# Retention outputs turned by VectorE, stored by ScalarE and gated in the last stage; a chunk's states first

## The chip, the cores and the metric

The kernel runs on one core of one Trainium2 chip. The metric is device time in microseconds, lower is better. A core has engines that run their own instruction queues in order and wait for each other through semaphores: TensorE (PE; its weight loads are listed as PEld), VectorE (DVE), ScalarE (ACT), GpSimd (POOL) and SyncE (SP), which here issues most DMA transfers.

## The reference

One layer of a hybrid decoder for a prompt of 1024 tokens and 32 sampled tokens (8 sequences of 4), all float32. The part that matters here is the retention branch, 4 heads with keys of 256 and values of 512, over the prompt in chunks of 128 tokens:

```python
def retention_chunk(q, k, v, s_prev, log_g):
    ...
    scores = jnp.einsum('bihd,bjhd->bhij', q, k) * dmask[None]
    intra = jnp.einsum('bhij,bjhe->bihe', scores, v)
    ...
    cross = jnp.einsum('bihd,bhde->bihe', q, s_prev) * q_decay[None, :, :, None]
    ...
    s_new = (jnp.exp(c * log_g)[None, :, None, None] * s_prev
             + jnp.einsum('bjhd,bjhe->bhde', k * k_decay[None, :, :, None], v))
    return intra + cross, s_new

def retention_out(o, rg, gn_w):
    ...
    on = ((o - mu) * lax.rsqrt(var + EPS)).reshape(b, s, RET_VW).astype(rg.dtype)
    return on * gn_w * jax.nn.silu(rg)
```

The gated outputs go through a projection (`w_down_ret`) and are merged with the attention branch by sigmoid gates; an output projection, a residual and a second gated embedding follow.

## The kernel before

Each float32 product is computed as three matmuls of rounded halves (`mac`, L265 to L269): high by high, high by low, low by high. Every operand is therefore split, usually by a copy on ScalarE or GpSimd (`hi_pool`, L197) for the high half and a subtraction on VectorE (`lo_of`, L200) for the low half. TensorE is kept busy by weaving streams of matmuls: a generator yields the cost of what it has just emitted, and `woven` takes turns by those costs. The final order of the instructions on each engine is set by a scheduler from dependences and priorities.

The stages by time: projections and gates (0 to about 370 us; the retention gate, after its SiLU, goes to DRAM as `gtD`), the paged attention of the sampled tokens (to 745), retention (745 to 1320), the prompt's attention (to 1620), and the last stage, which projects both branches, merges them and ends the layer.

In retention, a head's `prompt_chunks` (L926 to L1023) goes over eight chunks. `values_of` (L877) makes a chunk's values: 24 matmuls of 128x512 into the buffer `mm` (two PSUM buffers), then `vnh` on ScalarE (L884) and `vnl` on VectorE (L200). `front` (L935) makes the scores (L939), masks them (`smr`, L942), splits them (`smh`, `sml`) and loads and splits the decayed keys (`knh`, `knl`). `back` (L957) makes the output `po` of the chunk: three inner-chunk matmuls (values by scores), six on the old state (`Sth`, `Stl` by the split queries `qch`, `qcl`), then two sets of three for the new state, whose result is added to `S` (L981) and split into `Sth` (GpSimd) and `Stl` (VectorE) for the next chunk. `group_norm` (L887 to L903) normalises `po`: `bn` and its aggregate, `gv`, then `gr` on GpSimd, `gs`, `gb`, and `on` on ScalarE (L902).

`gate_out` (L910) turns the 128x512 `on` on TensorE, by four transposes of 128x128 into PSUM (L915), or for the sampled tokens by a matmul with a selecting matrix (L917), multiplies by the weight and the gate, which SyncE loaded (`gate_in`, L905), in four VectorE operations (L919), and stores the result with SyncE to `goD` (L921). In a head's loop, the values of chunk c+1 are woven with what is left of chunk c−1 (the `due` generator) and the first part of chunk c, with budgets 5.5 and 3.9.

`sample_state` (L1037) does the same for the sampled tokens with 16 states; its `gate_out` is done at the start of the next head (`late`). While one head's chunks end, the next head's `head_qk` (L816) projects queries and keys and copies them out on ScalarE.

In the last stage, `gated` (L1476) loads 128 rows of `goD` over all 1056 tokens, and `split_gated` splits them into `gh` (ScalarE) and `gl` (VectorE, three pieces of 352). `w4` is a pool of three buffers of 128x1056, used for the sigmoid gates (L1493) and later for other things. The products of this stage are evacuated by VectorE, one 128x352 piece each 24 matmuls (L1510, L1515, and L1532 on).

Of the kernel before, what the change touches and what calls it, by code (L numbers as in the profile page):

```python
# [162 lines left out]
def decode_step(ctx: ExitStack, tc: tile.TileContext, A: dict, O: dict):  # L163
# [17 lines left out]
    def tr():  # L181
        return banks["pool"].tile([P, 512], F32, tag="tr", name="tr", bufs=3)
# [13 lines left out]
    def hi_pool(out, src):  # L196
        pool.tensor_scalar(out, src, 1.0, 1.0, op0=ALU.mult, op1=ALU.mult)  # L197
# [22 lines left out]
    gtD, goD = ([dram.tile([P, 4, NT], F32, tag=f"{n}{h}", name=f"{n}{h}") for h in range(HR)] for n in ("gt", "go"))  # L220
# [684 lines left out]
    def gate_in(h, n, cols):  # L905
        g = p4.tile([P, 4, P], F32, tag="g", name="g", bufs=3)[:, :, :n]
        sp.dma_start(g, gtD[h][:, :, cols])
        return g

    def gate_out(h, on, n, cols, g):  # L910
        pt = tr()
        for f in range(4):
            o = pt[:, f * P:f * P + n]
            if n == P:
                pe.transpose(o, on[:, f * P:(f + 1) * P], ident)  # L915
            else:
                pe.matmul(o, on[:, f * P:(f + 1) * P], C("sel"), start=True, stop=True)  # L917
        for f in range(4):
            dve.scalar_tensor_tensor(out=g[:, f, :], in0=pt[:, f * P:f * P + n], scalar=gnw[:, 4 * h + f:4 * h + f + 1],  # L919
                                     in1=g[:, f, :], op0=ALU.mult, op1=ALU.mult)  # L920
        sp.dma_start(goD[h][:, :, cols], g)  # L921
# [4 lines left out]
    def prompt_chunks(h, X):  # L926
# [30 lines left out]
        def back(c, parts):  # L957
            sl = slice(c * P, (c + 1) * P)
            smh, sml, kh, kl = parts
            vh, vl = V.pop(c)  # L960
            if c:
                qh, ql = pair("qc", DK, 1)
                for m in range(2):
                    ms = slice(m * P, (m + 1) * P)
                    hi_pool(qh[:, ms], q[m][:, sl])
                    lo_of(ql[:, ms], q[m][:, sl], qh[:, ms])
            g = gate_in(h, P, sl)
            po = ac()
            mac(po, (smh, sml), (vh, vl), True, c == 0)
            yield 0.65  # L970
            for m in range(2 if c else 0):
                Sh, Sl = T["S"]
                ms, vs = slice(m * P, (m + 1) * P), slice(m * DV, (m + 1) * DV)
                mac(po, (qh[:, ms], ql[:, ms]), (Sh[:, vs], Sl[:, vs]), False, m == 1)
                yield 0.65
            for m in range(2):
                ms, vs = slice(m * P, (m + 1) * P), slice(m * DV, (m + 1) * DV)
                pS = ac()
                mac(pS, (kh[:, ms], kl[:, ms]), (vh, vl), True, True)
                if c:  # L980
                    dve.scalar_tensor_tensor(out=S[:, vs], in0=S[:, vs], scalar=gC, in1=pS, op0=ALU.mult, op1=ALU.add)  # L981
                else:
                    act.copy(S[:, vs], pS)
                yield 0.65
            if c < 7:
                Sh, Sl = T["S"] = tuple(p4.tile([P, 2 * DV], F32R, tag="st", name=f"St{n}", bufs=4) for n in "hl")
                for m in range(2):
                    vs = slice(m * DV, (m + 1) * DV)
                    hi_pool(Sh[:, vs], S[:, vs])
                    lo_of(Sl[:, vs], S[:, vs], Sh[:, vs])  # L990
            on = group_norm(po, P, C("qd", h, 1), C("qd2", h, 1))
            yield None
            gate_out(h, on, P, sl, g)
            yield 0.43

# [10 lines left out]
        while late:  # L1006
            gate_out(*late.pop())
        due = iter(())
# [28 lines left out]
    def sample_state(h, X):  # L1037
# [3 lines left out]
        sl = slice(SEQ, NT)  # L1041
# [30 lines left out]
        yield 2.5  # L1072
# [28 lines left out]
        g = gate_in(h, NR, sl)  # L1101
# [24 lines left out]
        if h + 1 < HR:  # L1126
            late.append((h, on, NR, sl, g))
        else:
            gate_out(h, on, NR, sl, g)
            yield 0.5  # L1130
# [350 lines left out]
    def split_gated(hi, lo):  # L1481

        for j in range(3):
            sl = slice(j * TH, (j + 1) * TH)
            split(b32(lo)[:, sl], hi[:, sl], lo[:, sl])
        return hi, lo

    def load_gated(f, pl):
        lo = gated(f, pl)
        return split_gated(pl("gh"), lo)  # L1490
# [30 lines left out]
    gx[7] = split_gated(xr_("gh"), gx[7])  # L1521
# [298 lines left out]
```

## Time and profile before

| | |
|---|---|
| time, median of 3 runs | 2126.42 us (2119.92 to 2126.49) |
| the profiled execution: time, span | 2122.66 us, 2120.9 us |
| granted TensorE clock | 0.997 of full speed |
| TensorE busy in 745 to 780, 855 to 905 and 905 to 980 us | 35.00 of 35, 50.00 of 50, 75.00 of 75 |
| turning transposes (L915) | 128 instructions, 19.3 us busy |
| selecting matmuls (L917) | 32 records of 269 ns (two for each instruction) |
| gating operations of 128x128 (L919) | 128 instructions, 341 ns each |
| `on` (L902), `vnl` (L200) | 36 of 778 ns, 32 of 686 ns |
| load of the gate, store of the result, to landing | 3.2 us and 2.6 us for 256 KB |
| TensorE's listed waits in all | 18 causes, the longest 4.9 us, at the start |

A row of the timeline gives the start, the duration, the engine, the source line, the operation, output and inputs by the program's names, and in brackets how long the engine was idle before it and what ended that. Matmuls are pipelined: durations overlap, and it is the distance between starts that adds up. [...] A row of the groups ends with busy time, mean nanoseconds of one, and the idle time before such instructions with its releasers. A row of the windows gives the stretch, its length, the busy time and count of PE, PEld, DVE, ACT and POOL, the granted clock, the DMA share and GB/s.

### The profile page before, as it was taken

To read this page: it belongs to the slowest core of one execution; us is meant where nothing else is said; L and a number is where in the kernel's file an instruction comes from. 1 tells how busy PE (TensorE), PEld (TensorE's weight loads), DVE (VectorE), ACT (ScalarE), POOL (GpSimd) and SP (SyncE) were. 2 spreads that over 40 slices of the span, in tenths; PEclk is the share of its full clock that TensorE was granted. 3 is DMA by queue.
4 is the path that set the end of the run, shared out by engine and by line. 5 is a ranking of instruction groups with operands and counts; after the bars stand their busy time and mean duration, and the time that the engine had idled before them with its cause. 6 is when DMAs were issued, how large, how long until landed. Compare 5 with 4: busy or idle time off the path is not lost. (4 is left out here: it accounts for less than half of the span.)

```text
span 2120.9 us, 38551 instructions
## 1 busy us (share of the span) xinstructions
PE 2085.8 (98%) x15282; PEld 1806.3 (85%) x15282; DVE 1239.0 (58%) x2791; ACT 699.6 (33%) x1455; POOL 306.0 (14%) x517
## 2 busy tenths in 40 slices
PE   8999999999999999999999999999999999999998
PEld 7988777777777898888888887888888999999976
DVE  6524555565655457677676774877777353454443
ACT  6312232333433232222222222454566341232221
POOL 2210111111100022222222220122211000000000
PEclk9999999999999999999999999999999999999999
DMA  7576656566565332654635647210112453336642
GB/s 206 135 242 212 238 193 233 208 246 227 193 240 182 113 87 71 206 163 140 208 87 163 195 147 251 56 48 19 39 52 81 152 181 94 95 117 133 175 151 91
DMA packets 346870, 321.91 MB, mean 152 GB/s; under 512 B 126945, under 2 KB 294049, under 8 KB 342593
## 3 DMA queue, kind: packets, MB, share of 16 engines
q1 hardware_dynamic: 320192, 213.92, 34.5%
q0 software_dynamic: 9216, 83.89, 10.6%
q10 hardware_dynamic: 17280, 21.63, 2.8%
q8 instruction: 120, 1.97, 0.4%
q14 instruction: 62, 0.50, 0.1%
HBM read 246.69 MB, written 72.69 MB: 151 GB/s over the span
## 5 line engine op out<-in xcount | busy, mean ns | idle before, releaser
L267 PE MATMUL mm<-xh,wh 128*128 128x352 f32 x1344 | 456.7, 340 | 3.9 <-ACT gev L440 2.3
L269 PE MATMUL mm<-xh,wl 128*128 128x352 f32 x1344 | 436.5, 325 | 2.1 <-DVE wl L200 2.1
L268 PE MATMUL mm<-xl,wh 128*128 128x352 f32 x1344 | 436.6, 325 | 0.0
L267 PEld LDWEIGHTS mm<-xh,wh 128*128 128x128 f32 x1344 | 253.2, 188 | 87.4 <-issue 77.2
L269 PEld LDWEIGHTS mm<-xh,wl 128*128 128x128 f32 x1344 | 254.2, 189 | 3.9 <-DVE wl L200 2.4
L268 PEld LDWEIGHTS mm<-xl,wh 128*128 128x128 f32 x1344 | 254.3, 189 | 3.4 <-issue 2.1
L688 DVE STREAM_TRANSPOSE kt<-craw 128x512 f32<-128x512 f32 x256 | 161.3, 681 | 85.9 <-PE sc L692 81.1
L200 DVE TENSOR_TENSOR wl<-wr,wh 128x512 fp32r<-128x512 f32 (+2 forms) x203 | 139.3, 699 | 98.1 <-ACT wh L248 67.1
L248 ACT CAST wh<-wr 128x512 fp32r<-128x512 f32 x150 | 90.0, 618 | 240.5 <-PE mm L268 184.6
L440 ACT ACTIVATE gev<-mm 128x352 f32<-128x352 f32 x120 | 55.5, 463 | 238.8 <-PE mm L269 218.4
L267 PE MATMUL mm<-mh,wh 128*128 128x352 f32 x384 | 124.5, 324 | 1.4 <-ACT mh L1197 0.8
L268 PE MATMUL mm<-ml,wh 128*128 128x352 f32 x384 | 124.8, 325 | 0.8 <-DVE ml L200 0.6
L269 PE MATMUL mm<-mh,wl 128*128 128x352 f32 x384 | 124.3, 324 | 0.0
L269 PE MATMUL mm<-gh,wl 128*128 128x352 f32 x384 | 124.3, 324 | 0.0
L267 PE MATMUL mm<-gh,wh 128*128 128x352 f32 x384 | 124.3, 324 | 0.0
L268 PE MATMUL mm<-gl,wh 128*128 128x352 f32 x384 | 124.2, 323 | 0.0
L267 PE MATMUL mm<-wv,xh 128*128 128x512 f32 x256 | 103.5, 404 | 0.0
L268 PE MATMUL mm<-wv,xh 128*128 128x512 f32 x256 | 100.9, 394 | 0.0
L269 PE MATMUL mm<-wv,xl 128*128 128x512 f32 x256 | 100.8, 394 | 0.0
L692 PE MATMUL sc<-kt,q 32*32 32x512 f32 x2560 | 91.2, 600 | 0.0
L902 ACT ACTIVATE on<-ac,gb,gs 128x512 f32<-128x512 f32 x36 | 28.0, 778 | 153.1 <-DVE gb L900 147.9
L267 PEld LDWEIGHTS mm<-mh,wh 128*128 128x128 f32 x384 | 72.4, 188 | 1.9 <-ACT mh L1197 1.0
(419 smaller groups left out, 4365.6 us busy)
## 6 DMA issues: line engine op xcount, KB each, us to landing
wr<-in_w_in_dram SPq DMA_DIRECT2D x144, 256.0 KB, 3.7
st<-in_state_ret_dram SPq DMA_DIRECT2D x32, 512.0 KB, 5.1
out_ret_sample_dram<-st SPq DMA_DIRECT2D x32, 512.0 KB, 3.5
gt<-gev ACTq DMA_DIRECT2D x48, 176.0 KB, 3.1
gl<-go SPq DMA_DIRECT2D x16, 528.0 KB, 5.4
gate<-ga SPq DMA_DIRECT2D x16, 528.0 KB, 3.6
g<-gt SPq DMA_DIRECT2D x32, 256.0 KB, 3.2
go<-g SPq DMA_DIRECT2D x32, 256.0 KB, 2.6
```

What stands on the lines that cost most here:

```text
L200: dve.tensor_tensor(out=out, in0=src, in1=b32(hi), op=ALU.subtract)
L248: hi_by[0](hi, raw)
L267: pe.matmul(out, wh, xh, start=first, stop=False)
L268: pe.matmul(out, wh, xl, start=False, stop=False)
L269: pe.matmul(out, wl, xh, start=False, stop=last)
L440: act.activation(t, ps, func)
L688: dve.transpose(kt[:, 2 * i + s].rearrange("p (n r) -> p n r", r=32), src)
L692: pe.matmul(sc[32 * v:32 * v + 32, q, :], Q["q4"][qs_, j + v // 2, 2 * (g % 2) + v % 2, :], kt[qs_, v, :], start=n == 0, stop=n == NJ // 2 ...
L902: act.activation(on[:n], po, AF.Identity, bias=nb[:n], scale=s[:n])
```

## The change

1. `gate_in` and `gate_out` go. `turn_out` lets VectorE transpose `on` in blocks of 32x32 (one stream transpose of 128x512 from SBUF to SBUF), and `store_out` lets ScalarE store it in four transfers, one for each 32 tokens, in pieces of 128 bytes. `goD` has a layout that fits these blocks. TensorE, the PSUM buffer `tr` and SyncE take no part any more.
2. The store of a chunk is emitted one chunk later: `store_out` stands ahead of `turn_out`.
3. The gate is applied in the last stage: `gated` loads the rows of `goD` and the gate `rg` (a buffer of `w4`), and VectorE multiplies them with the weight over 128x1056 ahead of the split. 16 such loads and 16 such operations are new.
4. In `back` the matmuls for the new state come first, then the inner-chunk and the old-state matmuls for the output. The old state's halves are kept in `old`.
5. `front(1)`, the scores and keys of the second chunk, is emitted inside the woven loop of the first chunk, once its costs have passed 3.5. The budget of the chunk's remainder goes from 3.9 to 3.5, and a yield in `sample_state` from 2.5 to 3.5.

```diff
-    gtD, goD = ([dram.tile([P, 4, NT], F32, tag=f"{n}{h}", name=f"{n}{h}") for h in range(HR)] for n in ("gt", "go"))
+    gtD = [dram.tile([P, 4, NT], F32, tag=f"gt{h}", name=f"gt{h}") for h in range(HR)]
+    goD = [dram.tile([DV // 32, 32, NT], F32, tag=f"go{h}", name=f"go{h}") for h in range(HR)]
...
-    def gate_in(h, n, cols):
...
-    def gate_out(h, on, n, cols, g):
...
+    def turn_out(h, on, n, t0):
+        st = p4.tile([P, DV], F32, tag="g", name="g", bufs=3).rearrange("p (b r) -> p b r", r=32)
+        dve.transpose(st, on.rearrange("p (b r) -> p b r", r=32))
+        turned_out.append((h, st, n, t0))
+
+    def store_out():
+        while turned_out:
+            h, st, n, t0 = turned_out.pop(0)
+            for a in range(4):
+                act.dma_start(goD[h][:, :, t0 + a * n:t0 + a * n + n].rearrange("b i t -> i b t"), st[32 * a:32 * a + 32, :, :n])
...
-            g = gate_in(h, P, sl)
-            po = ac()
-            mac(po, (smh, sml), (vh, vl), True, c == 0)
-            yield 0.65
-            for m in range(2 if c else 0):
-                Sh, Sl = T["S"]
...
+            old = T.get("S")
             for m in range(2):
                 pS = ac()
...
+            po = ac()
+            mac(po, (smh, sml), (vh, vl), True, c == 0)
+            yield 0.65
+            for m in range(2 if c else 0):
+                Sh, Sl = old
...
             on = group_norm(po, P, C("qd", h, 1), C("qd2", h, 1))
             yield None
-            gate_out(h, on, P, sl, g)
-            yield 0.43
+            store_out()
+            turn_out(h, on, 32, c * P)
...
-                parts = front(c + 1)
-                yield 1.0
-                yield from woven((chain(due, ahead(u)), 3.9), (values_of(c + 1, X, V), 5.5))
+                if c:
+                    parts = front(c + 1)
+                    yield 1.0
+                both = woven((chain(due, ahead(u)), 3.5), (values_of(c + 1, X, V), 5.5))
+                for cost in both:
+                    yield cost
+                    if c == 0:
+                        done += cost
+                        if done > 3.5:
+                            parts, done = front(1), -99.0
+                            yield 1.0
...
-        yield 2.5
+        yield 3.5
...
         lo = pl("gl")
-        sp.dma_start(b32(lo), goD[f // 4][:, f % 4, :])
-        return lo
+        sp.dma_start(b32(lo), goD[f // 4][4 * (f % 4):4 * (f % 4) + 4].rearrange("b i t -> (b i) t"))
+        g = w4("rg", dt=F32)
+        sp.dma_start(g, gtD[f // 4][:, f % 4, :])
+        dve.scalar_tensor_tensor(out=g, in0=b32(lo), scalar=gnw[:, f:f + 1], in1=g, op0=ALU.mult, op1=ALU.mult)
+        return lo, g
```

TensorE's order in the middle of a head, from a chunk's scores on (`ac<-q,k`). Before, the transposes stand behind the scores, then the inner-chunk matmuls between values (`mm`) of the next chunk:

```order
3680 L939 MATMUL ac<-q_7994,k_8230 128x128
3681 L939 MATMUL ac<-q_7995,k_8231 128x128
3682 L915 MATMUL tr<-cst,on 128x128 x4
3683 L267 MATMUL mm<-wv,xh_113 128x512
3684 L268 MATMUL mm<-wv,xh_113 128x512
3685 L269 MATMUL mm<-wv,xl_114 128x512
3686 L267 MATMUL ac<-vnh,smh 128x512
3687 L268 MATMUL ac<-vnl,smh 128x512
3688 L269 MATMUL ac<-vnh,sml 128x512
```

Now, in the same place (`mac` stands one line lower, and the middle matmul of a product need not follow the first directly):

```order
3637 L935 MATMUL ac<-q_7994,k_8230 128x128
3638 L935 MATMUL ac<-q_7995,k_8231 128x128
3639 L268 MATMUL mm<-wv,xh_113 128x512
3640 L269 MATMUL mm<-wv,xh_113 128x512
3641 L268 MATMUL ac<-vnh,knh 128x512
3642 L270 MATMUL mm<-wv,xl_114 128x512
3643 L268 MATMUL mm<-wv,xh_115 128x512
3644 L269 MATMUL ac<-vnl,knh 128x512
3645 L270 MATMUL ac<-vnh,knl 128x512
```

The transposes are gone, and the state matmuls (`knh`) are the first to use `vnh` and `vnl`; the inner-chunk matmuls (`smh`) follow later. Of a product's three matmuls the one with `vnl` is put a few places back.

VectorE's order around the end of a chunk's output, in the middle of a head. Before, from the group norm's first operation on:

```order
593 L890 BN_STATS st_8890<-ac 128x6
594 L200 TENSOR_TENSOR qcl<-q_7994,qch 128x128
595 L892 BN_AGGR mv<-st_8890 128x2
596 L200 TENSOR_TENSOR qcl<-q_7995,qch 128x128
597 L894 TENSOR_SCALAR gv<-mv,cst 128x1
598 L981 SCALAR_TENSOR_TENSOR S<-S,ac 128x512
599 L898 TENSOR_TENSOR gs<-gr,cst 128x1
600 L900 SCALAR_TENSOR_TENSOR gb<-mv,gs 128x1
601 L200 TENSOR_TENSOR Stl<-S,Sth 128x512
602 L981 SCALAR_TENSOR_TENSOR S<-S,ac 128x512
603 L942 TENSOR_TENSOR smr<-ac,cst 128x128
604 L200 TENSOR_TENSOR vnl<-mm,vnh 128x512
```

Now:

```order
577 L891 BN_STATS st_8771<-ac 128x6
578 L200 TENSOR_TENSOR qcl<-q_7994,qch 128x128
579 L893 BN_AGGR mv<-st_8771 128x2
580 L200 TENSOR_TENSOR qcl<-q_7995,qch 128x128
581 L895 TENSOR_SCALAR gv<-mv,cst 128x1
582 L899 TENSOR_TENSOR gs<-gr,cst 128x1
583 L901 SCALAR_TENSOR_TENSOR gb<-mv,gs 128x1
584 L938 TENSOR_TENSOR smr<-ac,cst 128x128
585 L200 TENSOR_TENSOR vnl<-mm,vnh 128x512
586 L910 STREAM_TRANSPOSE g<-on 128x512
587 L200 TENSOR_TENSOR sml<-smr,smh 128x128
588 L963 SCALAR_TENSOR_TENSOR S<-S,ac 128x512 x2
```

The updates of the state `S` and its low half have moved from the middle of the group norm to behind `vnl`, and the new transpose stands right behind `vnl`.

ScalarE's order over one chunk in the same place, before (`on` of a chunk, then the casts of the next):

```order
573 L902 ACTIVATE on<-ac,gb,gs 128x512
574 L884 CAST vnh<-mm 128x512
575 L943 CAST smh<-smr 128x128
576 L953 ACTIVATE knh<-knl,cst 128x256
577 L902 ACTIVATE on<-ac,gb,gs 128x512
```

And now:

```order
578 L885 CAST vnh<-mm 128x512
579 L903 ACTIVATE on<-ac,gb,gs 128x512
580 L939 CAST smh<-smr 128x128
581 L917 DMA go_102<-g 32x16x32 x3
582 L949 ACTIVATE knh<-knl,cst 128x256
583 L917 DMA go_102<-g 32x16x32
584 L885 CAST vnh<-mm 128x512
```

`vnh` has moved ahead of `on`, and four stores stand behind `smh`, three of them ahead of `knh`.

More of the change, by code (lines that the diff above doesn't have):

```diff
@@ L903, in group_norm @@
         return on
-    def gate_in(h, n, cols):
-        g = p4.tile([P, 4, P], F32, tag="g", name="g", bufs=3)[:, :, :n]
-        sp.dma_start(g, gtD[h][:, :, cols])
-        return g
-    def gate_out(h, on, n, cols, g):
[L911 to L921, printed above, removed]
+    turned_out = []
+    def turn_out(h, on, n, t0):
[7 more added lines that the diff above has]
+                act.dma_start(goD[h][:, :, t0 + a * n:t0 + a * n + n].rearrange("b i t -> i b t"), st[32 * a:32 * a + 32, :, :n])
     def pair(name, w, bufs, rows_=P):
@@ L1006, in prompt_chunks @@
         while late:
-            gate_out(*late.pop())
-        due = iter(())
+            turn_out(*late.pop())
+        due, done = iter(()), 0.0
         for c in range(8):
@@ L1126, in sample_state @@
         if h + 1 < HR:
[L1127 removed]
+            late.append((h, on, NS * 2, SEQ))
         else:
[L1129 to L1130 removed]
+            store_out()
+            turn_out(h, on, NS * 2, SEQ)
+            store_out()
     HB = 4
```

30 lines of the change are left out of this document (14 added, 16 removed).

## The prediction

> **What bounds the kernel now.** I read the page's first part, then the engines by stage (the windows), then the list of what TensorE waits for, and last the timeline of one steady chunk of the retention stage on each engine.
>
> ```profile
> PE 2085.8 (98%) x15282; PEld 1806.3 (85%) x15282; DVE 1239.0 (58%) x2791; ACT 699.6 (33%) x1455; POOL 306.0 (14%) x517
> ...
> 780.00:855.00 75.00, 74.40 (x353) 61.01 (x352) 54.41 (x140) 19.44 (x39) 19.60 (x37) 1.00 0.32 79
> 1620.00:1800.00 180.00, 179.37 (x1112) 179.13 (x1112) 79.16 (x153) 58.41 (x100) 2.84 (x6) 1.00 0.45 147
> ...
> PE tr L915 <- ACT on L902: 0.5, 1, 0.5
> PE tr L917 <- ACT on L902: 0.4, 1, 0.4
> ```
>
> TensorE is busy 98% of the span. In the window rows the columns are length, then PE, PEld, DVE, ACT and POOL busy, the granted clock, the DMA share and GB/s: in the retention window (780 to 855) and in the last stage (1620 to 1800) TensorE has no gap to speak of at a clock of 1.00, while VectorE works 54.41 of 75 and 79.16 of 180 us. Of the waits on the code that changes only two, of 0.5 and 0.4 us, are listed. So a microsecond is won here only by taking an instruction from TensorE, and lost by any wait that is put into its queue. The change does both, and the sum is the difference.
>
> **What leaves TensorE.** 128 transposes of the prompt chunks (32 sets of four, L915) and 16 small selecting matmuls (four sets, L917).
>
> ```profile
> 805.83 0.60 PE L939 MATMUL ac<-q,k 128*128 128x128 f32 x4
> ...
> 806.51 0.39 PE L268 MATMUL mm<-wv,xh 128*128 128x512 f32 x1
> ...
> 816.54 0.60 PE L939 MATMUL ac<-q,k 128*128 128x128 f32 x4
> ...
> 817.65 0.40 PE L268 MATMUL mm<-wv,xh 128*128 128x512 f32 x1
> ```
>
> The first column is the start; starts are what counts, since ends overlap. From the scores (L939) to the second values matmul pass 0.68 us without transposes (805.83 to 806.51) and 1.11 us with a set between (816.54 to 817.65): a set costs 0.43 us. 23 of the 32 sets stand next to the scores.
>
> ```profile
> 806.97 0.40 PE L267 MATMUL ac<-vnh,smh 128*128 128x512 f32 x1
> 807.91 0.65 PE L915 MATMUL tr<-cst,on 128*128 128x128 f32 x4 [0.54 <-ACT on L902]
> 808.32 0.48 PE L268 MATMUL ac<-vnl,smh 128*128 128x512 f32 x1
> 808.63 0.40 PE L269 MATMUL ac<-vnh,sml 128*128 128x512 f32 x1
> ...
> 924.91 0.98 PE L917 MATMUL tr<-cst,on 128*128 128x32 f32 x8
> 925.72 0.69 PE L939 MATMUL ac<-q,k 128*128 128x128 f32 x4
> ```
>
> A set by itself takes 0.41 us to the next matmul (807.91 to 808.32), and that one's successor comes after 0.31 instead of 0.23 (the pitch from 822.09 to 822.32 below): 0.49 us, for 9 sets. A selecting set takes 0.81 us (924.91 to 925.72), four of them. Waits that vanish with their instruction: 0.71 us at 806.97 to 807.91 (0.94 less one pitch), 0.2 at 797.16 (below), and about 0.6 at the last selecting set, taken from the listed 0.4 plus a restart. Sum: 23 x 0.43 + 9 x 0.49 + 4 x 0.81 + 1.5 = 9.9 + 4.4 + 3.2 + 1.5 = 19.0 us. VectorE is not the path in these windows, so that it loses its gating operations and gains a transpose per chunk counts only through the chain that follows.
>
> **What is put in: a wait of TensorE for `vnl`.** In the new order a chunk's state matmuls come right behind its values and scores, so the low half of the values (`vnl`, VectorE's subtraction) is wanted earlier. On VectorE it stands in the queue behind the whole group norm of the chunk before: bn, qcl, aggr, qcl, gv, gs, gb, smr, then vnl. Before the change it was wanted only by the inner-chunk matmuls, behind further values.
>
> ```profile
> 822.09 0.40 PE L269 MATMUL ac<-Sth,qcl 128*128 128x512 f32 x1
> 822.32 0.40 PE L267 MATMUL mm<-wv,xh 128*128 128x512 f32 x1
> ...
> 822.52 0.70 DVE L890 BATCH_NORM_STATS2 st<-ac 128x6 f32<-128x512 f32 x1 [2.19 <-PE ac L269]
> 823.59 0.21 DVE L894 TENSOR_SCALAR gv<-mv,cst 128x1 f32<-128x1 f32 x1
> 824.50 0.15 DVE L898 TENSOR_TENSOR gs<-gr,cst 128x1 f32<-128x1 f32 x1
> 824.69 0.61 DVE L900 SCALAR_TENSOR_TENSOR gb<-mv,gs 128x1 f32<-128x1 f32 x1
> 827.12 0.29 DVE L942 TENSOR_TENSOR smr<-ac,cst 128x128 f32<-128x128 f32 x1 [0.45 <-PE ac L939]
> 827.33 0.68 DVE L200 TENSOR_TENSOR vnl<-mm,vnh 128x512 fp32r<-128x512 f32 x1
> ...
> 824.67 0.62 POOL L197 TENSOR_SCALAR Sth<-S 128x512 fp32r<-128x512 f32 x1 [0.24 <-DVE gs L898]
> ...
> 918.71 0.16 DVE L900 SCALAR_TENSOR_TENSOR gb<-mv,gs 128x1 f32<-128x1 f32 x1
> 918.89 0.53 DVE L845 TENSOR_TENSOR rt<-k,sinR 128x352 f32<-128x352 f32 x1
> ```
>
> Both sides on one clock, from the last matmul on the old state (822.09). TensorE, new order: six values from 822.32 at 0.233 (to 823.72), scores and one value 0.68 (824.40), one value (824.63, where `vnh` enters), two more matmuls behind it and one value: `vnl` is wanted at 822.32 + 6 x 0.233 + 0.68 + 4 x 0.233 = 825.33. VectorE: the chain bn to gs is bound by TensorE and GpSimd's `gr`, so gs starts at 824.50 as now and gb at 824.69. How long gb takes decides the rest. It takes 0.61 us here, while GpSimd's `Sth` runs (824.67 to 825.29), and 0.16 at 918.71, with GpSimd idle. In the new order `Sth` follows the state matmuls, so it comes after gb, and I take 0.16, its successor starting 0.18 behind it: smr 824.87, vnl 0.21 later (827.12 to 827.33) at 825.08, done 0.68 later at 825.76.
>
> [...]
>
> ```profile
> 797.16 0.39 PE L267 MATMUL ac<-vnh,smh 128*128 128x512 f32 x1
> 797.60 0.50 PE L268 MATMUL ac<-vnl,smh 128*128 128x512 f32 x1
> 797.94 0.39 PE L269 MATMUL ac<-vnh,sml 128*128 128x512 f32 x1
> ...
> 796.86 0.69 DVE L200 TENSOR_TENSOR vnl<-mm,vnh 128x512 fp32r<-128x512 f32 x1 [0.35 <-ACT vnh L884]
> ...
> 826.25 0.39 PE L269 MATMUL mm<-wv,xl 128*128 128x512 f32 x1
> ...
> 826.67 0.58 ACT L884 CAST vnh<-mm 128x512 fp32r<-128x512 f32 x1 [0.50 <-PE mm L269]
> ```
>
> What a wait for `vnl` costs beyond its end is seen at 797: vnl ends at 797.55, the matmul starts at 797.60 and the next 0.34 behind it, 0.11 over the pitch. So the steady chunk waits 825.76 + 0.05 + 0.11 - 825.33 = 0.6 us. The short distance holds in 14 chunks (third to seventh of heads 0 and 3, sixth and seventh of heads 1 and 2), 8.4 us; in the same two heads the third and fifth have one or two matmuls more between, 1.3 us together. `vnh` is no wait of its own there: it starts 0.42 behind the last value (826.25 to 826.67) and ends before 824.63 on that clock.
>
> Two kinds of chunks I can only bound. In the last chunk of each head `vnl` stands behind casts of the next head's weights: with one such 0.68 operation ahead of it, 0 to 0.7, I take 0.6, 2.5 us over four. In the second chunk ScalarE's queue has `on` of the first chunk ahead of `vnh`, and `on` waits for the group norm behind the rotary work on keys that was moved there: zero if VectorE comes early, 2 us if three of that work's operations, of 0.53 us as at 918.89, come first; I take 1.2, 4.8 over four. Sum of new waits: 9.7 + 2.5 + 4.8 = 17.0 us, from 9 (steady ones alone) to 27 (long gb and the upper bounds).
>
> **What lies beside other work.**
>
> ```profile
> L688 DVE STREAM_TRANSPOSE kt<-craw 128x512 f32<-128x512 f32 x256 | 161.3, 681 | 85.9 <-PE sc L692 81.1 <-DMA q4D<-sel 4.7
> ...
> 840.25 0.56 SPq L921 DMA_DIRECT2D go<-g  x1
> ...
> L1397 DVE TENSOR_TENSOR mla<-mla,mg 128x1056 f32<-128x1056 f32 x7 | 8.8, 1252 | 0.1
> ...
> kD<-kb SPq DMA_DIRECT2D x64, 44.0 KB, 1.7
> gl<-go SPq DMA_DIRECT2D x16, 528.0 KB, 5.4
> ...
> q1 hardware_dynamic: 320192, 213.92, 34.5%
> ...
> 1661.43 0.52 DVE L1515 TENSOR_TENSOR M<-mm,gate 128x352 f32<-128x352 f32 x1 [3.35 <-PE mm L269]
> 1665.36 0.52 DVE L1515 TENSOR_TENSOR M<-mm,gate 128x352 f32<-128x352 f32 x1
> ```
>
> The turn is a 128x512 stream transpose, 0.68 us (L688), on VectorE behind `vnl`: from 825.76 to 826.4. Then ScalarE issues four stores at 0.56 us (the store of today, 840.25, has as many pieces), to 828.7, with `knh` between them and the next `vnh` behind. That one starts 1.9 us into the next chunk, at about 834, so some 5 us are to spare: nothing. SyncE loses 36 loads and 36 stores in this stage and gains 16 loads later: nothing. The queue's mean packet is 34.5% x 2120.9 x 16 / 320192 = 37 ns; the stores become 65,536 pieces of 128 bytes where 32,768 of 512 bytes were loaded and stored, about 33,000 more, 33,000 x 37 ns / 16 = 76 us over a stage of 540: 0.14 on a share of 0.32 to 0.68. Nothing.
>
> In the last stage each of 16 multiplications takes about 1.25 us (L1397, the same shape), 20 us on a VectorE that is busy 79 of 180. Its place is between two evacuations of the product, 3.9 us apart (1661.43 to 1665.36, with two PSUM buffers), waiting for loads of 5.4 us issued at the end of the product before; with 1.25 behind that the evacuation is late by under 2 us and the second buffer covers 3.9. Nothing; if a load takes 3 us more, about 1 us for that product.
>
> **Sum.** 2122.66 - 19.0 + 17.0 = 2120.7 us, against the profiled execution's own time. The median of before is 2126.42, 3.8 above that execution, and the lowest run 2119.92, 2.7 below it; so I give 2121 and count changes from 2122.66.
>
> **Rivals.** *The waits don't bite.* If VectorE brings `vnl` some 0.6 us earlier, or the two bounded kinds cost nothing, the removed instructions show: 2122.66 - 19.0 = 2103.7 with no wait, 2113 with the steady ones alone. For it: the bounds of 7.3 us are mine. Against: gs at 824.50 hangs on TensorE and GpSimd, which the change leaves where they are. 0.36 for all that ends below 2116.3.
>
> *The stores hold ScalarE (slower).* ScalarE works in order; the first store of a chunk waits for the turn, and `knh` and the next `vnh` queue behind. It decides from the point at which four stores hold the queue 5 us longer than 2.2, that is 1.8 us each instead of 0.56. Half a microsecond past that in each of 28 chunks is 14 us: 2134.7. Against: 44 KB in 128-byte pieces land in 1.7 us today (kD<-kb). The long gb, +7 us, gives 2127.7 alone and joins this case with the upper bounds, 2131. 0.22. [...]
>
> *No net effect*, the forecast: 0.42.
>
> **How the numbers follow.** About 0.3%, 6.4 us, is what a measurement of this kernel can tell from nothing: below 2116.3 is faster, above 2129.0 slower. The range takes in two thirds of the first rival and most of the second: 2106 to 2133.
>
> **What would show it.** Right: in the steady chunk TensorE lists a wait of 0.4 to 0.7 us for `vnl` on VectorE, over 20 times; gb is 0.16; the chunk's period stays near 9.9 to 10.1 us; no wait for a store; the window of the last stage is unchanged. Wrong: no `vnl` wait and a period of 9.5 (first rival); ScalarE's `vnh` late behind its stores, or a wait at the heads' changes (second); TensorE below 99% in the last stage.

## The result and the profile after

The changed kernel takes 2135.03 us (median of 6 runs, 2133.44 to 2138.67) and the kernel before 2121.43 us (6 runs): a ratio of 1.0061, interval 1.0046 to 1.0075. Run again on another chip it gave 1.0067 (1.0053 to 1.0081). It is slower, by 13.6 and 13.8 us in medians, where no net effect was forecast.

The page's first part, the two windows shown of before, and the listed waits of TensorE between 780 and 1330 us (us in total, times, longest), all of the kernel after:

```profile
PE 2079.9 (97%) x15122; PEld 1785.9 (84%) x15122; DVE 1231.2 (58%) x2699; ACT 695.6 (33%) x1455; POOL 311.6 (15%) x517
...
780.00:855.00 75.00, 72.74 (x324) 57.05 (x323) 49.71 (x118) 18.08 (x38) 22.32 (x39) 1.00 0.27 51
1620.00:1800.00 180.00, 176.17 (x1090) 173.41 (x1089) 102.26 (x183) 58.95 (x107) 4.28 (x8) 1.00 0.57 184
...
PE ac L268 <- ACT vnh L885: 8.9, 8, 1.7
PE ac L269 <- DVE vnl L200: 4.8, 10, 1.1
PE tr L1090 <- ACT vs L1087: 2.3, 3, 1.1
PE ac L1079 <- DMA wvS<-in_w_in_dram: 1.2, 2, 0.9
```

TensorE has 160 instructions fewer and is busy 5.9 us less, yet the span is 13.6 us longer: it now waits. In the same stretch before, 1.2 us of waits were listed (0.5, 0.4 and 0.3, besides two of 1.0 that belong to the next stage); now it is 17.2, and the matmul behind a stalled one comes up to 0.1 us late as well (below).

To place the loss I cut both executions at events that both have. From the first chunk score to the last `on` (rows of one operation: count, duration in ns, first and last start; the 64 score products stand as 128 records):

```profile
L939 PE MATMUL ac<-q,k x128: 270/275/356, 781.2 to 1259.0; 128*128 128x128 f32 x128
L902 ACT ACTIVATE on<-ac,gb,gs x36: 777/778/781, 793.6 to 1318.3; 128x512 f32<-128x512 f32 x36
```

```profile
L935 PE MATMUL ac<-q,k x128: 270/275/348, 779.8 to 1267.9; 128*128 128x128 f32 x128
L903 ACT ACTIVATE on<-ac,gb,gs x36: 777/778/785, 795.8 to 1327.8; 128x512 f32<-128x512 f32 x36
```

The upper rows are of before, the lower of after. Before: 1318.3 - 781.2 = 537.1 us; after: 1327.8 - 779.8 = 548.0. So 10.9 of 13.6 us are lost in retention. Cut the same way, the stage's end (last `on` to the first matmul on the attention's `pth`) grows from 39.8 to 41.6 us, and the last stage (first to last evacuation, `M` to `mev`) from 271.7 to 274.4.

Within retention the starts of the scores split it (a period runs from one chunk's scores to the next chunk's): over four heads the first two periods lose 4.2 us, the third period 6.1, the next four gain 2.2, the stretches between two heads and to the last `on` lose 2.8.

**The steady chunk** is what was forecast. TensorE, then VectorE, after:

```profile
826.40 0.48 PE L268 MATMUL ac<-vnh,knh 128*128 128x512 f32 x1
826.95 0.40 PE L268 MATMUL mm<-wv,xh 128*128 128x512 f32 x1
827.45 0.50 PE L269 MATMUL ac<-vnl,knh 128*128 128x512 f32 x1
827.78 0.40 PE L270 MATMUL ac<-vnh,knl 128*128 128x512 f32 x1
...
826.43 0.16 DVE L901 SCALAR_TENSOR_TENSOR gb<-mv,gs 128x1 f32<-128x1 f32 x1
826.71 0.68 DVE L200 TENSOR_TENSOR vnl<-mm,vnh 128x512 fp32r<-128x512 f32 x1
827.50 0.71 DVE L910 STREAM_TRANSPOSE g<-on 128x512 f32<-128x512 f32 x1
```

vnl ends at 827.39, the matmul on it starts at 827.45: 0.50 behind its predecessor, 0.27 over the pitch of 0.233. The matmuls behind vnh and vnl add 0.09 and 0.10 (restarts). In all 0.46 us against the 0.43 of a set of transposes: the period is 9.97 us, where it was 9.94 to 9.95. gb takes 0.16 us, as taken. In the fifth and sixth periods of heads 1 and 2 nothing waits, and they take 9.50 to 9.52 us.

**The first chunk of heads 1 to 3** was taken as nothing in the forecast. TensorE, ScalarE (ACTq rows are DMA issues) and VectorE at head 1:

```profile
926.57 0.50 PE L268 MATMUL ac<-vnh,knh 128*128 128x512 f32 x1 [0.82 <-ACT vnh L885]
928.63 0.50 PE L269 MATMUL ac<-vnl,knh 128*128 128x512 f32 x1 [1.10 <-DVE vnl L200]
...
921.79 0.78 ACT L903 ACTIVATE on<-ac,gb,gs 128x512 f32<-128x512 f32 x1 [6.62 <-DVE gb L901]
922.98 0.45 ACT L842 COPY rx<-mm 128x352 f32<-128x352 f32 x1
923.96 1.93 ACTq L917 DMA_DIRECT2D go<-g  x4
925.93 0.58 ACT L885 CAST vnh<-mm 128x512 fp32r<-128x512 f32 x1 [1.68 <-DMA go<-g]
...
927.03 0.97 DVE L857 STREAM_TRANSPOSE kb<-k 128x352 f32<-128x352 f32 x2 [1.04 <-POOL k L851]
927.92 0.65 DVE L200 TENSOR_TENSOR vnl<-mm,vnh 128x512 fp32r<-128x512 f32 x1
```

ScalarE issues the late sample's four stores (1.93 us) right ahead of vnh; then vnl stands behind the turning of this head's keys (`kb`), which waits for GpSimd's `k`. GpSimd's step needs, by way of VectorE, the product that ScalarE copies out as `rx`, and `rx` stands behind the late sample's `on`, which starts 3.43 us after the head's first score (918.36).

**The second chunk** waits for vnh, which stands behind `on`, which waits for the group norm:

```profile
937.95 0.50 PE L268 MATMUL ac<-vnh,knh 128*128 128x512 f32 x1 [1.69 <-ACT vnh L885]
...
936.65 0.78 ACT L903 ACTIVATE on<-ac,gb,gs 128x512 f32<-128x512 f32 x1 [1.52 <-DVE gb L901]
937.33 0.57 ACT L885 CAST vnh<-mm 128x512 fp32r<-128x512 f32 x1
```

**The stage's end.** By the row of `lh`, the next stage's first tile, ScalarE stood until the last turned output had landed. TensorE's wait, 1.0 us before (and 1.0 more, for `ll`, a little later), is 2.4 (the releaser named, a DMA, had been done). Behind it the granted clock falls, to 0.58 over the 4 us shown (0.99 in the 8 us ahead):

```profile
1333.95 0.58 PE L268 MATMUL ac<-wqr,lh 128*128 128x256 f32 x1 [2.41 <-DMA mg<-gev]
...
1329.31 2.10 ACTq L917 DMA_DIRECT2D go<-g  x4
1333.49 1.85 ACT L1214 CAST lh<-lat 128x256 fp32r<-128x256 f32 x5 [1.45 <-DMA go<-g]
...
1334.00:1338.00 4.00, 4.00 (x16) 3.73 (x17) 3.92 (x10) 3.95 (x9) 1.10 (x3) 0.58 0.55 151
```

### The profile page after: what moved, and what is told of

Same layout as the page of the kernel before. It is cut to its first block, busy times and chain, and to the rows that moved or that the text cites. A ratio compares the mean times of both kernels' runs of the same rounds, so it can differ in the third digit from the quotient of the medians.

```text
span 2134.5 us, 38260 instructions
## 1 busy us (share of the span) xinstructions
PE 2079.9 (97%) x15122; PEld 1785.9 (84%) x15122; DVE 1231.2 (58%) x2699; ACT 695.6 (33%) x1455; POOL 311.6 (15%) x517
## 3 DMA queue, kind: packets, MB, share of 16 engines
q0 software_dynamic: 9216, 83.89, 10.5%
## 4 chain that ended last, share of the span: by engine, by line
PE 76%; DVE 7%; DMA 6%; issue 5%; POOL 3%; ACT 2%; SPq 0%; ACTq 0%; POOLq 0%; DVEq 0%
PE mm L268 18%; PE mm L270 17%; PE mm L269 17%; PE sc L693 4%; PE x L724 3%; DMA wr<-in_w_in_dram 2%; PE ac L269 2%; PE ac L270 2%; PE ac L268 2%; PE mm L1386 2%; DMA gl<-go 1%; PE tr L1372 1%; DVE st L891 1%; POOL gr L897 1%; PE ac L1329 1%
## 5 line engine op out<-in xcount | busy, mean ns | idle before, releaser
L269 PEld LDWEIGHTS mm<-ml,wh 128*128 128x128 f32 x384 | 72.3, 188 | 1.5 <-DVE ml L200 1.4
```

Of the source, the lines that this page charges most:

```text
L269: pe.matmul(out, wh, xl, start=False, stop=False)
```

## The experiments

My theory was that waits put into TensorE's queue eat the transposes' gain: the vnl behind the group norm, the second chunk's keys, and the stores on ScalarE. The rivals: one of these alone, the order of the work itself, or the gating in the last stage. Ratios are to the kernel before on the same chip; R is the stretch from the first chunk score to the last `on`, in one profile (before 537.1 us, after 548.0 and, run again, 546.2).

| kernel | median, us | before, us | ratio (interval) | R, us |
|---|---|---|---|---|
| changed kernel again | 2136.36 | 2122.56 | 1.0067 (1.0053 to 1.0081) | 546.2 |
| stores by SyncE | 2149.85 | 2131.64 | 1.0084 (1.0069 to 1.0098) | 553.6 |
| output first | 2134.05 | 2131.64 | 1.0017 (1.0006 to 1.0028) | 535.2 |
| second chunk's keys early | 2139.92 | 2131.64 | 1.0044 (1.0027 to 1.0060) | 545.5 |
| turn alone | 2147.82 | 2131.64 | 1.0080 (1.0065 to 1.0094) | 549.9 |
| no gate | 2144.40 | 2130.92 | 1.0062 (1.0046 to 1.0077) | 550.7 |
| vnl ahead | 2130.72 | 2130.92 | 0.9997 (0.9984 to 1.0010) | 532.0 |
| vnl ahead, again | 2119.94 | 2123.39 | 0.9981 (0.9968 to 0.9993) | 530.5 |
| vnl ahead, stores by SyncE | 2137.11 | 2130.92 | 1.0031 (1.0018 to 1.0044) | 543.7 |
| output first, stores by SyncE | 2144.91 | 2130.92 | 1.0070 (1.0048 to 1.0092) | 551.2 |
| before, states first | 2132.19 | 2122.56 | 1.0040 (1.0026 to 1.0054) | 545.2 |
| vnl ahead, stores behind vnh | 2128.07 | 2122.56 | 1.0029 (1.0016 to 1.0041) | 540.7 |
| the same, and room at the end | 2126.51 | 2122.56 | 1.0017 (1.0003 to 1.0030) | 537.8 |
| the same without room, keys' turn behind vnl | 2132.31 | 2123.39 | 1.0041 (1.0026 to 1.0056) | 543.6 |
| the same, and room at the end | 2132.17 | 2123.39 | 1.0042 (1.0026 to 1.0058) | 545.2 |

**The control.** The changed kernel once more:

> The changed kernel itself, once more, beside the three others on one chip. The edits so far were set against it across chips by their ratios to the kernel before; if that is fair, its ratio is again 1.005 to 1.008 (11 to 17 us over before). If it comes out under 1.003 or over 1.010, the ratios of the edits tell less than they seemed to.

It did. Its profile shows how far one profile is to be trusted: here the first chunk of head 1 has no wait (10.46 us between scores instead of 12.91), the stage's end loses 1.2 us instead of 1.8, at a granted clock of 1.00, and the last stage takes 271.7 us as before the change, at the same ratio. ScalarE at its head 1, whose first score starts at 919.78:

```profile
920.32 0.78 ACT L903 ACTIVATE on<-ac,gb,gs 128x512 f32<-128x512 f32 x1 [3.72 <-DVE gb L901]
921.50 0.46 ACT L842 COPY rx<-mm 128x352 f32<-128x352 f32 x1
922.49 1.94 ACTq L917 DMA_DIRECT2D go<-g  x4
926.23 0.59 ACT L885 CAST vnh<-mm 128x512 fp32r<-128x512 f32 x1 [3.45 <-PE mm L270]
```

The same four stores stand ahead of vnh, and nobody waits: `on` starts 0.54 us after the first score, not 3.43.

**The stores.** SyncE issues them instead of ScalarE.

```diff
-                act.dma_start(goD[h][:, :, ...
+                sp.dma_start(goD[h][:, :, ...
```

> The changed kernel with one edit: SyncE issues the stores instead of ScalarE. Theory (three separate queues each put a wait before TensorE; the stores on ScalarE are one of them): the waits for vnh in the first chunk of heads 1 to 3 (0.82, 0.83 and 0.33 us in the changed kernel) go, and of the 2.41 us at the end of the stage about 1.4 stays; the second chunk's waits for vnh (1.63 to 1.70) and the steady waits for vnl stay. Sum 3 to 5 us faster than the changed kernel, so 8 to 10 us slower than before. Rival A (the stores hold ScalarE in every chunk and are the whole loss): 12 us or more faster than the changed kernel, no slower than before. Rival B (the order of the states is the whole loss): no difference from the changed kernel, 13 us slower than before.

Half of it came: the first chunk of heads 1 to 3 fell to 10.5 us between scores; there the late sample's `on` starts 1.05 to 1.39 us after the first score. But the time rose, at each head's end: from the last score to the last `on` pass 68.6 us (60.2 in the changed kernel), and the stage's end waits 6.9 us. The same with vnl ahead (ScalarE keeps the stores of the stage's end) and with the output first:

```diff
-    def store_out():
+    def store_out(by=sp):
...
-            store_out()
+            store_out(act)
```

> The kernel of the edit before, with SyncE issuing all stores but those at the end of the stage, which ScalarE keeps. Theory: the first chunks of heads 1 to 3 lose their waits (2.45, 2.4 and 1.85 us in the profiles of the changed kernel against the one with stores by SyncE), and the 6.9 us at the end of the stage that SyncE's stores cost there do not come: 5 to 8 us faster than the edit before, 5 to 9 us faster than before the change. Rival (SyncE's queue is late for the loads of keys and weights once it has to wait for the turn): no faster than the edit before.

> The changed kernel with two edits: output before states, and SyncE issues all stores but those at the end of the stage. Theory: the 5.0 us that output first gained between the first and the last scores stay, the first chunks' waits of heads 2 and 3 (1.7 and 2.3 us) go: 3 to 7 us faster than before the change. Rival (the stores on SyncE cost what they save): as slow as with the output first alone, 2 to 6 us slower than before.

Both failed. SyncE's queue (vnl ahead, stores by SyncE), TensorE's wait at the end, and the window around it:

```profile
1274.68 6.13 SPq L922 DMA_DIRECT2D go<-g  x4
...
1292.47 13.66 SPq L1055 DMA_DIRECT2D wvS<-in_w_in_dram  x8
...
PE ac L268 <- ACT lh L1221: 7.5, 1, 7.5
...
1334.00:1344.00 10.00, 5.50 (x17) 4.68 (x18) 6.41 (x16) 5.49 (x12) 1.45 (x3) 0.50 0.45 97
```

Four stores occupy SyncE for 6.13 us, waits for the turn included, and the sample's weights and states, which SyncE loads behind them, come late (last score to last `on`: 69.7 us, 59.9 with ScalarE's stores). The end then waits 7.5 us, and the clock granted over the 10 us shown is 0.50. So SyncE is the worse place here, though ScalarE also computes (33% busy). That the loads behind the stores are the cause I read from the queue; no run moved the loads alone.

**The order.** Output first as before, all else changed:

> The changed kernel with one edit: the output's matmuls come before the new state's again, as before the change. Theory: the steady waits for vnl (0.27 to 0.33 us over the pitch, with two restarts of 0.09 and 0.10 beside them, 0.46 us in some 20 chunks) go, since the group norm then ends a state's six matmuls earlier; the first and second chunks keep most of their waits. Sum 6 to 10 us faster than the changed kernel, so 3 to 7 us slower than before. Rival A (stores): no difference from the changed kernel. Rival B (the order is the whole loss): 13 us or more faster than the changed kernel, as fast as before or faster.

```diff
+            po = ac()
+            mac(po, (smh, sml), (vh, vl), True, c == 0)
...
             for m in range(2):
...
                 mac(pS, (kh[:, ms], kl[:, ms]), (vh, vl), True, True)
...
-            po = ac()
-            mac(po, (smh, sml), (vh, vl), True, c == 0)
```

The time held by the ratio (3.6 us over before; 2.4 by the medians): 10 us or more of the 13.6 come back, and R is 535.2. The second chunk's waits, which I expected to stay, are gone, so they too came with the order. Then the order alone, in the kernel before, with TensorE's turning and the gate left:

> The kernel before with one part of the change alone: a chunk's states are multiplied ahead of its output; TensorE's turning, SyncE's store and the gate stay. My theory: the order costs only because vnl gets queued behind the group norm's gs and gb on VectorE, and here vnl is queued ahead of them, so the time is that of before, -2 to +3 us. Rival: the order itself costs, since the states' matmuls need vnh and vnl at the chunk's first step, whatever is queued: 5 to 10 us slower than before.

Here I was wrong, and the rival has the size, 9.6 us in medians. But the wait is another than either of us named:

```profile
PE tr L915 <- ACT on L902: 5.3, 8, 0.9
...
PE ac L268 <- DVE vnl L200: 0.2, 1, 0.2
```

With the states first the output is normalised later, and the old transposes wait for `on`. The changed kernel has no such transposes, so this run prices the order in the old kernel, not its share of the 13.6 us.

**vnl behind the group norm.** `gs` and `gb`, with them `on`, are issued behind the next chunk's vnl.

```diff
+        last_vnl[0] = dve.tensor_tensor(out=vl, in0=ps, in1=b32(vh), op=ALU.subtract)
...
-            on = group_norm(po, P, C("qd", h, 1), C("qd2", h, 1))
+            half = group_norm(po, P, C("qd", h, 1), C("qd2", h, 1))
             yield None
+            with tc.issue_after(last_vnl[0].ins):
+                on = norm_out(*half)
```

> The changed kernel with one edit: on VectorE the last two steps of a chunk's group norm (gs, gb) are put behind the next chunk's vnl, so that on comes behind the next vnh too. Same work, same stores, same order of the states. Theory (the states-first order loses because vnl and vnh queue behind the norm of the chunk before): the steady waits for vnl go (0.46 us with restarts in some 20 chunks) and the second chunks' waits for vnh (1.6 to 1.7 us) shrink to under 0.5; the first chunks of heads 1 to 3, the end of the stage and the last stage keep theirs. 11 to 16 us faster than the changed kernel, so between 3 us faster and 2 us slower than before. Rival (the states-first order costs by something else, such as the wait of the inner-chunk matmuls for on): the waits only move to the inner-chunk matmuls, and it is 8 us or more slower than before.

> The kernel with vnl ahead of gs once more, beside the two others on one chip and on another chip than before. If its draw with the kernel before was no accident of that chip, its ratio is again 0.998 to 1.001; the kernel whose stores go behind vnh came out 0.3% above it on another chip, and if chips and not the edits make that difference, it comes out at about 1.002 to 1.003 here.

It held twice (of the second chunks only head 0's still waits, 0.8 us), and the second time the kernel beat before: 0.9981 (0.9968 to 0.9993). VectorE and TensorE of its steady chunk, second run:

```profile
826.10 0.69 DVE L888 TENSOR_TENSOR vnl<-mm,vnh 128x512 fp32r<-128x512 f32 x1
...
826.91 0.15 DVE L904 TENSOR_TENSOR gs<-gr,cst 128x1 f32<-128x1 f32 x1
...
827.28 0.40 PE L268 MATMUL ac<-vnh,knh 128*128 128x512 f32 x1
827.52 0.39 PE L269 MATMUL ac<-vnl,knh 128*128 128x512 f32 x1
827.75 0.40 PE L270 MATMUL ac<-vnh,knl 128*128 128x512 f32 x1
```

No gap is left, the third period falls to 9.6 us in heads 1 to 3, and the fourth to seventh to 38.1 together from 39.7: 0.41 us each, the 0.43 of the transposes. In the second chunk `on` now stands behind vnh on ScalarE as well. What the group norm holds up is the largest part of the loss, shown by removing it. It is not all that eats the forecast's 19 us: retention is now 5.1 and 6.6 us shorter than before, but the stage's end (42.6 and 42.2 us, 39.8 before) and the last stage (274.1 and 274.4, 271.7 before) take back 5.2 and 5.1.

**The second chunk's keys** early again:

```diff
-                if c:
-                    parts = front(c + 1)
-                    yield 1.0
-                both = woven((chain(due, ahead(u)), 3.5), (values_of(c + 1, X, V), 5.5))
+                parts = front(c + 1)
+                yield 1.0
+                yield from woven((chain(due, ahead(u)), 3.5), (values_of(c + 1, X, V), 5.5))
```

> The changed kernel with one edit: the second chunk's scores and keys are begun with the first chunk's remainder again, not once 3.5 of cost have passed. Theory: the second chunk's waits for vnh (1.63, 1.69, 1.70 and 1.66 us, with restarts 7.4 in all) go or shrink to under 0.5 each, since the group norm of the first chunk then stands ahead of the rotary work; sum 4 to 7 us faster than the changed kernel, so 6 to 9 us slower than before. Rival C (the wait is that of on behind the inner-chunk matmuls, wherever the keys are begun): no difference.

By the ratio some 4 us came back, the lower end of the forecast, but the cause is not shown. The second chunk's waits became 1.60, 0.96, 0.35 and 0.41 us: unchanged in head 0, under 0.5 in heads 2 and 3. There the first two periods took 18.7 and 18.8 us (16.9 and 16.2 in the changed kernel), so vnh had more time; in the run without the gate, whose keys are late, the waits behind such first chunks are 0.64 and 0.63 as well. The late keys are at most a part of the cause.

**The turn alone** (stores by SyncE, output first, keys early, budget 3.9 as before):

> The changed kernel with three edits together: stores by SyncE, output before state, second chunk's keys early with the former budget of 3.9. What stays of the change is the turn on VectorE and the gate in the last stage. Theory: TensorE loses its 144 instructions (17.5 us and some waits) and gets back only what the last stage costs (2.6 us) and perhaps 2 us at the heads' changes: 12 to 15 us faster than before. Rival (the turn itself or the loads of the last stage cost TensorE time that is not seen as waits): between 5 us faster and no change.

The largest miss. SyncE's stores bring their own price (above), here a wait of 5.8 us at the stage's end, besides 8.2 us of waits for vnl. No run has the turn with ScalarE's stores, early keys and the output first, so the turn's own price stays open.

**The gate** of the last stage:

```diff
-        g = w4("rg", dt=F32)
-        sp.dma_start(g, gtD[f // 4][:, f % 4, :])
-        dve.scalar_tensor_tensor(out=g, ...
-        return lo, g
+        return lo, b32(lo)
```

> The changed kernel without the gate in the last stage: its 16 loads and 16 multiplications are left out, and the retention outputs go into the projection without weight and gate. Theory: the stage from the first evacuation of the last stage to its last comes back from 274.4 to 271.7 us, the waits of 0.73 and 0.77 us there go, and nothing else changes: 2 to 4 us faster than the changed kernel, 9 to 11 us slower than before. Rival (the loads of the last stage and their buffers are the main loss): 8 us or more faster than the changed kernel.

This run leaves out the gate's work, so its outputs are others. No gain in the median. Its last stage takes 271.7 us, as in the two kernels that gate in retention (before, and before with states first). In the fourteen profiles with the gate it takes 271.7 to 276.1: the gate costs 0 to 4.4 us there, 1.9 in the mean, and does not explain the loss.

**What still holds the mended kernel.** The stores behind the next vnh, then the last turned output in a buffer of the weight loader, then the keys' turn behind vnl (with two rooms for the rotation's products, two for the turned output):

```diff
+            with tc.issue_after(last_vnh[0].ins):
+                store_out()
...
-        st = p4.tile([P, DV], F32, tag="g", ...
+        st = (room or p4).tile([P, DV], F32, tag="wr" if room else "g", ...
...
+            with tc.issue_after(last_vnl[0].ins):
+                for turn_third in X["kb"]:
+                    turn_third()
```

> The kernel with vnl ahead of gs, and besides each ScalarE store behind the next chunk's vnh, so that the four stores of the late sample no longer stand ahead of a head's first vnh. My theory: the first chunk of heads 1 to 3 falls from 12.3 to 13.0 us between scores to about 10.5, in all 6 us, and the whole to 4 to 8 us under before (ratio 0.996 to 0.998). Rival: vnl of those chunks still waits for the turned keys behind GpSimd, as its wait of 1.1 us showed, and only 1 to 3 us come back.

> The same, and the last sample's turned output lies in a buffer of the weight loader, so that the next stage's first tiles don't wait in its memory until the last store has landed. My theory: the wait for lh at the stage end (2.6 us, with 1.7 us at half clock behind it) goes, another 3 to 4 us: 7 to 12 us under before. Rival: the weight loads that now stand behind the sample's state stores come late, and a wait for wh of 1 to 4 us takes its place: no better than the kernel without this edit.

> vnl ahead of gs, stores behind vnh, and besides the turning of a head's second and third part of keys behind the first vnl of heads 1 to 3 (with two rooms for the rotation's products and two for the turned output, which that needs). My theory: the first vnl was late because VectorE stood at the turned keys, which wait for GpSimd; its waits of 2.4 to 2.8 us go with the half clock behind each, and the first chunk falls to about 10.5 us between scores in heads 1 to 3. In all 8 to 11 us under the kernel with the stores behind vnh: ratio 0.997 to 0.999 to before. Rival: the keys of the second chunk, which are read back after the turning, come late and hold the second chunk by as much: no better than 1.002.

> The same, and the last sample's turned output in a buffer of the weight loader. That edit gave 1.6 us in medians (0.1%) where it was tried first; the same here, ratio 0.996 to 0.998. Rival: nothing, since the next stage then waits for its weights.

All four forecasts missed. With the stores behind vnh, vnh comes in time in the first chunk, and TensorE then waits longer for vnl, by the wait that the rival had named. TensorE and VectorE at head 2:

```profile
1058.80 0.39 PE L270 MATMUL mm<-wv,xl 128*128 128x512 f32 x1
1061.36 0.50 PE L269 MATMUL ac<-vnl,knh 128*128 128x512 f32 x1 [2.17 <-DVE vnl L888]
...
1063.09 0.63 PE L269 MATMUL mm<-wv,xh 128*128 128x512 f32 x1
1063.52 0.63 PE L270 MATMUL mm<-wv,xl 128*128 128x512 f32 x1
...
1059.76 0.97 DVE L857 STREAM_TRANSPOSE kb<-k 128x352 f32<-128x352 f32 x2 [1.04 <-POOL k L851]
1060.65 0.65 DVE L888 TENSOR_TENSOR vnl<-mm,vnh 128x512 fp32r<-128x512 f32 x1
```

One gap of 2.2 us stands where there were two of 0.8 and 1.1, and behind it matmuls come at 0.43 us instead of 0.23. With the keys' turn behind vnl, ScalarE waits in its place, 1.17 and 0.47 us at two copies of the same keys ahead of vnh, again for GpSimd (the second is shown):

```profile
924.95 0.22 ACT L871 COPY kS<-k 128x32 f32<-128x32 f32 x1 [0.47 <-POOL k L851]
925.07 0.58 ACT L891 CAST vnh<-mm 128x512 fp32r<-128x512 f32 x1
...
PE ac L268 <- ACT vnh L891: 7.4, 3, 2.5
```

So the wait comes through whichever engine queues vnh or vnl behind GpSimd's rotation of the keys.

What makes the rotation late can be read across the runs, though none of them moved it. I compare heads 1 to 3 (33 starts of a head) in the eleven profiles of kernels that begin the second chunk's keys late and leave the keys' turn in its place. In the 24 with a wait, `rx` is copied 3.56 us or more after the head's first score; in the nine without one, within 2.25 us. ScalarE's stores are not needed for it: with output first and SyncE's stores, heads 1 and 2 wait (first chunks of 12.07 and 14.35 us). Why the late sample's `on`, ahead of `rx`, starts so late in most of them stays open; the longer yield in `sample_state` (part 5 of the change) was not tried by itself.

A buffer at the end gave 0.0012 of ratio in one pair (intervals overlap) and nothing in the other; TensorE's wait for `lh` was still 1.9 and 2.3 us, so the landing of the last output is not all of it.

## Why the prediction was wrong

Stretch by stretch, what the forecast's terms come to (with the removed instructions where they stood) and what one profile of each kernel shows, in us:

| stretch | forecast | measured |
|---|---|---|
| first two periods (three selecting sets leave) | -2.4 | +4.2 |
| third period (second chunk's wait) | +2.9 | +6.1 |
| fourth to seventh periods | -0.4 | -2.2 |
| between heads and to the last `on` | -0.7 | +2.8 |
| stage's end (one selecting set and its wait leave) | -1.4 | +1.8 |
| last stage | 0 | +2.7 |
| all else | 0 | -1.8 |
| sum | -2.0 | +13.6 |

The terms are of one profile; the control's split differs by up to 2.7 us in a term.

- *What leaves TensorE*, 19.0 us: right where it can be seen. Where nothing waits (vnl ahead) the steady chunk is 0.41 us shorter, 0.43 was taken; in the control's head 1, whose first chunk does not wait, the first two periods are 0.86 us shorter, 0.81 was taken.
- *A wait for vnl in the steady chunk*, 0.6 us: the mechanism and nearly the size, 0.46 with its restarts. That it lies behind the group norm is shown by taking it from there. TensorE lists only 0.15 to 0.30 us of it, seven times, where 0.4 to 0.7, over 20 times, was to be the sign. gb's 0.16 us came as taken: before, 28 of the 36 gb ran beside GpSimd's `Sth` and took 0.56 to 0.61 us, the other 8, without `Sth` beside them, 0.16; after, none of the 36 runs beside it, and all take 0.14 to 0.16. The 7 us for a long gb in the forecast's upper bounds (0.45 us, 0.61 less 0.16, in each of sixteen chunks) are an estimate, and no run of the new order shows them.
- The step that failed most is *"some 5 us are to spare: nothing"*. That spare time belongs to a steady chunk. At the start of heads 1 to 3 the late sample's `on`, its stores and the keys' rotation lie ahead of vnh and vnl, and the first two periods are 6.6 us over the forecast (5.3 in the control). There were three kinds of chunks, not two.
- *"Two kinds of chunks I can only bound"* failed in its size. The second chunk was put at 1.2 us within 0 to 2; the listed wait alone is 1.6 to 1.7, and the third period lost 6.1 us although it lost its transposes too, some 3 us more than the 4.8 taken. The bound nearly held; the value did not.
- *Between heads* the forecast had 5.6 us of transposes less and 4.9 us of waits more. Measured: 2.2 us lost over three stretches, 0.6 at the last. With vnl ahead these stretches take 276.5 and 274.8 us (before 277.1, after 279.8), so this is for the most part the same queue. TensorE's other listed waits there, 2.3 us for `vs`, which ScalarE copies behind casts that wait for weights, and 1.2 us for loads, go on in those runs (2.1 and 1.1, 1.4 and 1.3).
- *The last stage, "nothing"*: 2.7 us in this profile, 1.9 in the mean of all. The stage's end, whose new wait was not weighed at all: 3.2 us over the forecast (2.6 in the control).
- The rival named for the slower side, *the stores hold ScalarE*, has about the time (2131 to 2134.7) but not the reason: a chunk's four stores take 1.7 to 2.7 us of the queue, waits for the turn included, not the four times 1.8 at which it was to decide, and in the steady chunk nobody waits for them.

## What to carry to other kernels

When a change moves an operand's first use earlier, take every place where the loop meets something else (first, second and last round), and read there what stands ahead of its producer in its engine's queue: the steady round had been right to 0.15 us, and the edges decided. A wait that is mended at a queue may only uncover the next, on the same late chain: here the keys' rotation came through as a wait for ScalarE and VectorE, then VectorE alone, then ScalarE again. And an engine that computes nothing is not for that a free place for stores that wait: with them on SyncE, loads behind them, the kernel with vnl ahead went from 0.9997 to 1.0031 of before.

## What the runs showed of the hardware

In these runs some gaps cost more than themselves, and the length alone did not decide which. In the kernel with the stores behind vnh, the first chunks of heads 1 and 2 have the same wait, 2.18 and 2.17 us. TensorE's clock behind each (the third number from the end; the second head's matmul stands above):

```profile
923.87 0.50 PE L269 MATMUL ac<-vnl,knh 128*128 128x512 f32 x1 [2.18 <-DVE vnl L888]
924.50:928.00 3.50, 3.50 (x19) 2.94 (x18) 1.51 (x3) 1.18 (x2) 1.77 (x2) 1.00 0.47 79
1062.00:1065.50 3.50, 3.50 (x12) 2.75 (x11) 1.42 (x3) 1.18 (x2) 1.67 (x2) 0.58 0.47 79
```

The first went on at full clock, the second at half clock (matmuls 0.43 us apart instead of 0.23) for some 3 us, and its chunk took 14.18 us instead of 12.98. In the fifteen profiles of kernels with the turn on VectorE, between 780 and 1360 us, half clock follows none of 15 waits of 1.60 to 1.70 us, 21 of 27 of 1.77 to 2.78 us, and all four of over 5 us. Two shorter waits with a few matmuls between, 0.8 and 1.1 us, went without it in the changed kernel (head 2) and with it in the run without the gate (1.00 and 0.51 in the 3.5 us behind).

What decides between waits of one length is not shown. The half clock may add to the spread of one kernel's runs (2124.09 to 2136.99 with vnl ahead); that was not tested.
